# A hybrid decoder layer on one core: the 16-row solves of the chunk inverse along each partition's own row, in an order searched anew

## The chip, the core and the metric

The kernel runs on one core of a Trainium2 chip. A core has five engines with an instruction stream of their own each, which run their instructions in the order given: TensorE (PE, matrix products; PEld is its loading of weights), VectorE (DVE), ScalarE (ACT), GpSimd (POOL) and SyncE (SP), which here does nothing but issue transfers (DMA). The metric is the device time of one execution in microseconds (us). The profile and the trace come from one execution that the hardware profiler recorded.

## The reference

One layer of a decoder over 2048 tokens of width 1024 (`D_MODEL`). The token mixer is a gated DeltaNet of 8 heads of 128, next to a memory attention of 4 heads; then an output projection, two layer norms and a squared-ReLU MLP (1024 to 4096 and back). The part that the change touches is the chunked recurrence of the mixer:

```python
decay = jnp.exp(jnp.where(causal, gc[..., :, None] - gc[..., None, :], -jnp.inf))
lower = jnp.where(strict, jnp.einsum('bnhcd,bnhsd->bnhcs', k_beta, kc) * decay, 0.0)
a_mat = jnp.eye(CHUNK, dtype=f32) + lower
u = lax.linalg.triangular_solve(a_mat, v_beta, left_side=True, lower=True, unit_diagonal=True)
w = lax.linalg.triangular_solve(a_mat, k_beta * jnp.exp(gc)[..., None], left_side=True,
                                lower=True, unit_diagonal=True)
...
v_new = u_c - jnp.einsum('bhcd,bhde->bhce', w_c, state)
o = jnp.einsum('bhcd,bhde->bhce', qd, state) + jnp.einsum('bhcs,bhse->bhce', a_c, v_new)
state = state * dc[..., None, None] + jnp.einsum('bhcd,bhce->bhde', kd, v_new)
```

`q` and `k` are convolved, passed through SiLU and normalized per head; the output `o` is normalized by its root mean square and gated.

## The kernel before

The tokens go in four blocks of 512 (`TB`). In each block the mixer runs over the 8 heads, so that there are 32 pairs of block and head; `NC` = 4 chunks of 128 tokens make a block. Per pair, `dense` (L948) projects `cq`, `ck`, `cv` (products `aq`, `ak`, `av` of the input `T` with weights `whl`), convolves and gates them on DVE, squares them for the norms (`ss`) and works out small per-token factors on GpSimd: `rk`, `vbs`, `bh`, `nbe`, `e` (`e4`). `gdn_a` (L1125) makes the masked decays `dl` and `at` from `gb`, the products `pkq`, and multiplies them in, with `bh`; `invert` (L1004) inverts the four unit lower triangular 128x128 matrices I + L: first the 16-row blocks on the diagonal by substitution on DVE, then 16 to 32, 32 to 64 and 64 to 128 by pairs of small matmuls `pq` and `pp`, with the result in `Y`. `gdn_b` (L1183) runs the recurrence over the chunks (`pc`, `R`, `vt`, `po`, the state), then the norm (`oss`, `m`, `ro`), the transposition `pto` and the gate `cat`.

In the substitution the block's columns lie across partitions: `Lc` and `Xc` have 16 rows x 4 chunks along a partition. Step j spreads column j over a group of 16 partitions with a shuffle, multiplies it by one column of `Lc` and subtracts:

```python
for j in range(15):
    w = j + 1
    nc.vector.stream_shuffle(B[:, :w], Xc[:, :w], [j] * 16 + [16 + j] * 16)
    nc.vector.tensor_tensor(out=B[:, :w], in0=B[:, :w],
                            in1=Lc[:, j:j + 1].to_broadcast([P, w, NC]), op=ALU.mult)
    nc.vector.tensor_tensor(out=Xc[:, :w], in0=Xc[:, :w], in1=B[:, :w], op=ALU.subtract)
```

All large products are made of three fp32r matmuls on a high and a low part (`mm3`, the low parts by an ACT cast and a DVE subtract); the small ones of the inverse and the recurrence are fp32 matmuls. The out projection and the MLP use seven products for eight of half the size. The order in time is: mixer of blocks 0 and 1 (to about 640 us), out projection (to about 760), MLP (to about 1330), mixer of blocks 2 and 3 (from about 1390 to about 1940, about 1190 us of mixer in all), out projection (to about 2075), MLP (to the end).

Every operation of every engine is recorded first (`Recorder`) and then issued in the order of a table of numbers, `ORDER`, read by `order()` (L484) in `issue()` (L539), so that all of them have the line L549 in the trace. The table interleaves the pieces of a head with the projections of others, on each engine. Buffers come from pools of fixed number (four weight buffers `whl`, 14 slots of one kind for `gb`, `dl`, `at`, `Y` and the like); a transfer waits until its buffer is free.

Of the kernel before, what the change touches and what calls it, by code (L numbers as in the profile page):

```python
# [11 lines left out]
ALU = mybir.AluOpType  # L12
# [158 lines left out]
class Op:  # L171
# [4 lines left out]
    "c-rlK+m7ryuH+A;0qZXP|BsF0LfKiX*6!U8Gr$0iK4-72s!XS?3q=Nl!TZxb>Fa;vbCplke-?gmt@c^{bEO+U<$J%%e5d|8Cx5v1b@rduep%Y*"  # L176
    "!aJ^V^H1ed@TXGwRr{}H?Q87+>_6ah<&!3Uv0voIPw|&{cdq+(a=Ue{JO8-X=YLo4_;0E|e!p<L<Nd4sZJ(O=9kd%S^<Uh7>YuqEbDja&pWAQR"
    "cT#bC`_lWVu6<AY&dR<3o}$e0X}DO$jaG~jK3+0!yZ!ZcfBoP7bX^}`sEz$^FH_g5ciq3iNbhfIpS&<jt#DrUsO|sZZu6dteaHJ!_x$7XIsMa@"
    "UpberH?QB`wx=uafxh<F;tp2V{Pr8aZ=ZVeRy&uBK2p~HOeuBG?7kv~td4sR`ox3mk?o&eu~MdQV?PDHq@1s;{B6O^x5NS37p+=eHG9P--tLuj"
    "Ke^(5_IKgMzZ?4tUw~<@`$p=(eBWGjTH<vt0o?k``(ZKUcxTxIzjs0z{8oIX@8w%+;q~?#unjPIX|Mjob(gq#_WKJ~(tgN_B~ub-vGjuFv+p0*"  # L180
    "%9VQ%tDx*R=C*%V2EI<$ANz^17we~#j<5bNR@xpn4*H%lJx=F7%+rsCUk*%a&HK%G!P{sWslj>OPrX-o|7gSIS-p(*_Q53P#oNE~p6!fbyZ?*("
    "%lfC|rmlf~x9==3OuxRNW6NRs_YCb7MC;<o-wSc>5nM7Y*WL&FUHELCdn@DF@eEwKyvKn#n_(fkmOZDf?U8Qdr$O0^40{qQq{E1815+?JFhP4M"
    "VyrMpSp$Wiw^`Z0ygwuRseGZSEv%ogx%b6z+dcO$!?quwr}A2=xW`UI$ysUp`b8EO6S4;&-dynYnHGERn~}I`GjEE6muSugE%08G`%(9}?JwNB"
    "b?s~JEAMsnwj}$>_8-#T`>FG)^W0GUuQdMZZTiaVX)5Om_J8gb-|zsHyL{jO{{E%QH7=KoJ=gbl?0;ZSVSccCN*y{)_$e&^sr9&$c3kF7U->a^"
    "iP!sjmZ=*}`W-9|J|H{TxDxiy+z^vz*tKoU9?AjpHtxoIyc*8|O!ofnhQ~>Jv3Cw+;v(Q7um==_pZV|;AK`OuL)fr}_WC(52A1~NciLdv+cu=V"
    "$N26gsar4FYI~aaV*O#v*RyQ%`rY1Rt)+Zcb^E0LPg`>6*shq&H8g)%@%yItVYQkp2Y=Xi$=CZP_@HnawhOTh3|DQD3D;V#T;XF6H+IUzD#bHi"
    "_-D26qu{sO%2|h3{$W7I_t_R(2S-RQG%y_-pjTL#vhS_6ire2u()Kd;A;wJ!!v!OeCYD--(b<czby^4PttLC4ZklK8js2U<cf-Vwh3j#}FJ8Fe"
# [1885 lines left out]
```

## Time and profile before

| | us |
|---|---|
| runs | 2701.4, 2702.3, 2703.96 (median 2702.3) |
| profiled execution | 2702.34 |
| its span in the trace | 2700.6 |
| PE busy | 2679.2 (99%) |
| DVE busy | 2128.6 (79%) |
| ACT busy | 1640.6 (61%) |
| POOL busy | 425.8 (16%) |

The profiled execution's own time is 1.7 us more than its span, which runs from the first to the last instruction. Busy time is an average over stages with different limits, and an engine that is busy for less than the span may still be waited for at some places. The rows that matter stand below the change.

### The profile page before, as it was taken

To read this page: it belongs to the slowest core of one execution; us is meant where nothing else is said; L and a number is where in the kernel's file an instruction comes from. 1 tells how busy PE (TensorE), PEld (TensorE's weight loads), DVE (VectorE), ACT (ScalarE), POOL (GpSimd) and SP (SyncE) were. 2 spreads that over 40 slices of the span, in tenths; PEclk is the share of its full clock that TensorE was granted. 3 is DMA by queue.
4 is the path that set the end of the run, shared out by engine and by line. 5 is a ranking of instruction groups with operands and counts; after the bars stand their busy time and mean duration, and the time that the engine had idled before them with its cause. 6 is when DMAs were issued, how large, how long until landed. Compare 5 with 4: busy or idle time off the path is not lost.

```text
span 2700.6 us, 42572 instructions
## 1 busy us (share of the span) xinstructions
PE 2679.2 (99%) x13553; PEld 2248.0 (83%) x13553; DVE 2128.6 (79%) x5658; ACT 1640.6 (61%) x4128; POOL 425.8 (16%) x1023
## 2 busy tenths in 40 slices
PE   9999999999999999999999999999999999999998
PEld 7888888888888888888888888888888888888887
DVE  7999889998877776766788887999978666567485
ACT  7778767786575555333446777777756555544342
POOL 3233233331000000000012322332201000000011
PEclk9999999999999999999999999999999999999999
DMA  8767558877888888789785434545678654486673
GB/s 296 267 212 282 182 184 289 310 252 266 280 297 291 302 292 290 284 291 296 236 300 198 154 134 163 181 150 184 211 266 282 216 175 148 152 291 217 209 238 121
DMA packets 222896, 633.73 MB, mean 235 GB/s; under 512 B 25648, under 2 KB 34256, under 8 KB 203728
## 3 DMA queue, kind: packets, MB, share of 16 engines
q1 hardware_dynamic: 222240, 630.97, 67.9%
q8 instruction: 107, 1.75, 0.3%
q14 instruction: 117, 0.96, 0.1%
q10 hardware_dynamic: 432, 0.05, 0.0%
HBM read 446.83 MB, written 184.09 MB: 234 GB/s over the span
## 4 chain that ended last, share of the span: by engine, by line
PE 91%; DVE 4%; DMA 2%; ACT 1%; issue 1%; POOL 0%; SPq 0%; POOLq 0%; DVEq 0%; ACTq 0%
PE fA L549 13%; PE f2A L549 12%; PE ao L549 8%; PE f2C L549 6%; PE fC L549 6%; PE az L549 6%; PE av L549 6%; PE ak L549 6%; PE aq L549 5%; PE f2B L549 3%; PE fB L549 3%; PE pc L549 3%; PE amq L549 3%; PE po L549 2%; PE pkq L549 1%; PE pq L549 1%
## 5 line engine op out<-in xcount | busy, mean ns | idle before, releaser
L549 ACT CAST whl<-wraw 128x512 fp32r<-128x512 f32 (+2 forms) x294 | 225.9, 779 | 194.4 <-PE fC L549 54.2
L549 DVE TENSOR_TENSOR whl<-wraw,whl 128x512 fp32r<-128x512 f32 (+2 forms) x294 | 257.9, 887 | 95.0 <-ACT whl L549 90.1
L549 PE MATMUL fA<-B,whl 128*128 128x512 f32 x1152 | 291.4, 390 | 0.0
L549 PE MATMUL f2A<-whl,X 128*128 128x512 f32 x1152 | 264.7, 390 | 0.0
L549 PEld LDWEIGHTS fA<-B,whl 128*128 128x128 f32 x1152 | 216.4, 188 | 44.9
L549 PEld LDWEIGHTS f2A<-whl,X 128*128 128x128 f32 x1152 | 216.3, 188 | 44.8
L549 ACT CAST X<-X 128x1024 fp32r<-128x1024 f32 x118 | 123.2, 1050 | 171.4 <-DMA X<-xsc 129.5
L549 PE MATMUL av<-T,whl 128*128 128x512 f32 x768 | 224.7, 406 | 0.0
L549 PE MATMUL ak<-T,whl 128*128 128x512 f32 x768 | 220.2, 404 | 0.1
L549 PE MATMUL aq<-T,whl 128*128 128x512 f32 x768 | 217.3, 403 | 2.7 <-ACT whl L549 1.2
L549 DVE TENSOR_TENSOR X<-X,X 128x1024 fp32r<-128x1024 f32 x118 | 143.5, 1220 | 82.7 <-ACT X L549 82.6
L549 PE MATMUL fC<-B,whl 128*128 128x512 f32 x768 | 199.3, 390 | 0.0
L549 PE MATMUL az<-T,whl 128*128 128x512 f32 x624 | 182.2, 405 | 0.0
L549 PE MATMUL f2C<-whl,X 128*128 128x512 f32 x768 | 177.0, 390 | 0.9 <-ACT X L549 0.9
L549 POOL TENSOR_SCALAR ve<-mv 128x1 f32<-128x1 f32 x34 | 20.5, 602 | 983.9 <-DVE mv L549 975.3
L549 PEld LDWEIGHTS f2C<-whl,X 128*128 128x128 f32 x768 | 144.2, 188 | 31.1 <-ACT X L549 1.3
L549 ACT CAST whl<-whl 128x1024 fp32r<-128x1024 f32 x92 | 96.7, 1052 | 119.5 <-DMA whl<-tsc 84.4
L549 PEld LDWEIGHTS fC<-B,whl 128*128 128x128 f32 x768 | 144.2, 188 | 29.9
L549 PEld LDWEIGHTS aq<-T,whl 128*128 128x128 f32 x768 | 138.5, 189 | 29.1 <-DVE T L549 2.0
L549 PEld LDWEIGHTS ak<-T,whl 128*128 128x128 f32 x768 | 138.2, 189 | 23.4 <-ACT whl L549 0.5
L549 PEld LDWEIGHTS av<-T,whl 128*128 128x128 f32 x768 | 137.3, 189 | 21.3 <-ACT ck L549 0.2
L549 DVE TENSOR_TENSOR whl<-whl 128x1024 fp32r<-128x1024 f32 x92 | 112.0, 1220 | 48.8 <-ACT whl L549 48.6
(305 smaller groups left out, 6437.5 us busy)
## 6 DMA issues: line engine op xcount, KB each, us to landing
whl<-wsc SPq DMA_DIRECT2D x100, 1024.0 KB, 5.4
wraw<-in_w_ff_dram SPq DMA_DIRECT2D x106, 512.0 KB, 4.7
X<-xsc SPq DMA_DIRECT2D x96, 512.0 KB, 5.0
wsc<-whl SPq DMA_DIRECT2D x36, 1024.0 KB, 6.5
whl<-tsc SPq DMA_DIRECT2D x64, 512.0 KB, 4.7
xsc<-hB SPq DMA_DIRECT2D x96, 256.0 KB, 3.5
xo<-cat SPq DMA_DIRECT2D x80, 256.0 KB, 5.3
wraw<-in_w_in_dram SPq DMA_DIRECT2D x35, 512.0 KB, 4.4
```

Of the source, the lines that this page charges most:

```text
L549: o.fn(*[res(a) for a in o.args], **{k: res(v) for k, v in o.kw.items()})
```

## The change

`invert`: The 16-row substitution runs along each partition's own row. `Lc` now holds, on each partition, I - L of its own row of the block (4 chunks x 16); it is stored to DRAM (`lscr`) and loaded back as two tiles `Lr` of 128 x 512, in which every partition of a group of 16 has all 16 rows of its block. Step j then is a product `Mc` of row j with what is solved so far, and a sum over it, which is entry j: no shuffle and no subtraction. The result comes out transposed, so that `ZT` is built first and `Z` by a transposition of it.

`dense`: `bh` is worked out on DVE from `ss` and `ib` = 1 + exp(-b), as the reciprocal of their product, without the power `rk`; the additions of the epsilons are made apart for k and q, the one of q in one operation with its factor. `gdn_b`: the factor 1/P moves into the squares on ScalarE, and one GpSimd operation per head goes. The table `ORDER` is another one.

```diff
+    nhalf = cst.tile([P, 2], F32, name="nhalf")
+    nc.vector.tensor_scalar_mul(nhalf, half, -1.0)
...
-        nc.gpsimd.tensor_scalar_add(ss, ss, 4 * RMS_EPS)
+        bh = res["bh"] = small("bh", [P, NC])
+        nc.vector.scalar_tensor_tensor(out=bh, in0=ss[:, :NC].part(0), scalar=4 * RMS_EPS, in1=G["ib"][:, h], op0=ALU.add, op1=ALU.mult)
+        nc.vector.reciprocal(bh, bh)
         rk = small("rk", [P, NC])
-        nc.gpsimd.tensor_tensor(out=rk, in0=ss[:, :NC], in1=mhalf, op=ALU.pow)
-        res["e4"] = small("e4", [P, NC], 4)
-        nc.gpsimd.tensor_scalar_mul(res["e4"], ss[:, NC:], P * RMS_EPS)
+        nc.gpsimd.tensor_scalar_add(rk, ss[:, :NC].part(0), 4 * RMS_EPS)
+        nc.gpsimd.tensor_tensor(out=rk, in0=rk, in1=mhalf, op=ALU.pow)
...
-        bh = res["bh"] = small("bh", [P, NC])
-        nc.gpsimd.tensor_tensor(out=bh, in0=G["beta"][:, h], in1=rk, op=ALU.mult)
-        nc.gpsimd.tensor_tensor(out=bh, in0=bh, in1=rk, op=ALU.mult)
+        res["e4"] = small("e4", [P, NC], 4)
+        nc.gpsimd.tensor_scalar(out=res["e4"], in0=ss[:, NC:].part(1), scalar1=4 * RMS_EPS, scalar2=P * RMS_EPS, op0=ALU.add, op1=ALU.mult)
...
-        Lc = small("Lc", [P, 16, NC], 2)
-        Lf = Lq.rearrange("p c f -> p f c")
-        nc.vector.tensor_scalar_mul(Lc, Lf[:, 0:16], half[:, 0:1])
-        nc.vector.scalar_tensor_tensor(out=Lc, in0=Lf[:, 16:32], scalar=half[:, 1:2], in1=Lc,
+        Lc = small("Lc", [P, NC, 16], 2)
+        nc.vector.scalar_tensor_tensor(out=Lc, in0=Lq[:, :, 0:16], scalar=nhalf[:, 0:1],
+                                       in1=i16.unsqueeze(1).to_broadcast([P, NC, 16]), op0=ALU.mult, op1=ALU.add)
+        nc.vector.scalar_tensor_tensor(out=Lc, in0=Lq[:, :, 16:32], scalar=nhalf[:, 1:2], in1=Lc,
                                        op0=ALU.mult, op1=ALU.add)
...
-        for j in range(15):
+        lscr = rec.buf(dr, (8, 16 * 16 * NC), F32, "lscr", 2, "lscr")
+        nc.sync.dma_start(out=lscr.rearrange("g (i f) -> (g i) f", i=16), in_=Lc.rearrange("p c f -> p (c f)"))
+        Lr = []
+        for n in range(2):
+            t = slot("Lr", "s0")
+            nc.sync.dma_start(out=t, in_=lscr[:, n * TB:(n + 1) * TB].unsqueeze(1).to_broadcast([8, 16, TB]))
+            Lr += [t.rearrange("p (i c f) -> p i c f", i=8, c=NC)[:, m] for m in range(8)]
...
+        for j in range(1, 16):
             w = j + 1
-            nc.vector.stream_shuffle(B[:, :w], Xc[:, :w], [j] * 16 + [16 + j] * 16)
-            nc.vector.tensor_tensor(out=B[:, :w], in0=B[:, :w],
-                                    in1=Lc[:, j:j + 1].to_broadcast([P, w, NC]), op=ALU.mult)
-            nc.vector.tensor_tensor(out=Xc[:, :w], in0=Xc[:, :w], in1=B[:, :w], op=ALU.subtract)
+            nc.vector.tensor_tensor(out=M[:, :, :w], in0=Lr[j][:, :, :w], in1=Xc[:, :, :w], op=ALU.mult)
+            nc.vector.tensor_reduce(out=Xc[:, :, j], in_=M[:, :, :w], op=ALU.add, axis=AX.X)
...
-            nc.scalar.activation(j, p3[:, c], AF.Square, accum_out=o[:, c:c + 1])
+            nc.scalar.activation(j, p3[:, c], AF.Square, scale=P ** -0.5, accum_out=o[:, c:c + 1])
...
-        nc.gpsimd.tensor_scalar_mul(m4, oss, 1.0 / P)
-        nc.gpsimd.tensor_tensor(out=m4, in0=m4, in1=e4, op=ALU.add)
+        nc.gpsimd.tensor_tensor(out=m4, in0=oss, in1=e4, op=ALU.add)
```

How the instructions stand on an engine is shown at three places (the numbers behind the names count buffers). On DVE, in the middle of a solve early in the program, the order before has this, a step of three operations with pieces of the next head's convolution (`cq`), of the state and of `R` between them:

```order
L549 STREAM_SHUFFLE Bc_2398<-Xc_2255 128x16
L549 TENSOR_TENSOR Bc_2398<-Bc_2398,Lc_2886 128x16
L549 TENSOR_TENSOR kq_2844<-ck_2388,kq_2834 128x512
L549 SCALAR_TENSOR_TENSOR cq_2977<-raw_2495,cw_96,cq_2977 128x512
L549 SCALAR_TENSOR_TENSOR state_2889<-state_2889,el_513,pc_2960 128x128
L549 TENSOR_TENSOR Xc_2255<-Xc_2255,Bc_2398 128x16
L549 STREAM_SHUFFLE Bc_2398<-Xc_2255 128x20
```

Now, on DVE in the mixer of block 2, at the place where the least work stands between `Lc` (whose store follows it on SP) and the first product `Mc`, the order has:

```order
L579 SCALAR_TENSOR_TENSOR Lc_16619<-Lq_16562,nhalf_86,Lc_16619 128x64
L579 TENSOR_SCALAR Y_15779<-pp_16611 64x2x64
L579 SCALAR_TENSOR_TENSOR cq_16584<-raw_16332,cw_98,cq_16584 128x512 x2
L579 SCALAR_TENSOR_TENSOR cat_16669<-pto_16645,gnwh_94,cz_15540 128x512
L579 SCALAR_TENSOR_TENSOR cq_16584<-th_16657,cq_16584 128x512
L579 SCALAR_TENSOR_TENSOR ck_16667<-raw_16570,cw_98,ck_16667 128x512 x2
L579 SCALAR_TENSOR_TENSOR R_16717<-pc_16673,nbe_16111,vb_16648 128x128
L579 SCALAR_TENSOR_TENSOR bh_16719<-ss_16685,ib_14951 128x4
L579 SCALAR_TENSOR_TENSOR ck_16667<-raw_16570,cw_98,ck_16667 128x512
L579 TENSOR_TENSOR Mc_16742<-Lr_16664,Xc_16153 128x4x2
L579 TENSOR_REDUCE Xc_16153<-Mc_16742 128x4
L579 TENSOR_TENSOR Mc_16742<-Lr_16664,Xc_16153 128x4x3
```

A step is two operations now, and the first one of a head needs what SP loads. SP's order for the same head is this, with weights `whl` and a kept gate `cz` around the new transfers, where it had weights and kept gates alone:

```order
L579 DMA lscr_16630<-Lc_16619 128x64
L579 DMA Lr_16664<-lscr_16630 128x1x512
L579 DMA whl_16675<-wsc_2257 128x2048
L579 DMA cz_16682<-zsc_15580 128x512
L579 DMA Lr_16689<-lscr_16630 128x1x512
L579 DMA whl_16696<-wsc_2395 128x2048
```

The first load stands directly behind the store that it reads, and the weights behind both. At the start of the program, on PE, the order before begins with matmuls on constants (`warm`):

```order
L549 MATMUL warm_106<-ones_80 128x128 x7
L549 MATMUL aq_124<-T0_118,whl_120 128x512
L549 MATMUL aq_124<-T1_122,whl_120 128x512
L549 MATMUL aq_124<-T0_118,whl_120 128x512
L549 MATMUL warm_106<-ones_80 128x128 x2
```

and now with the first projection:

```order
L579 MATMUL aq_139<-T0_130,whl_134 128x512
L579 MATMUL aq_139<-T1_136,whl_134 128x512
L579 MATMUL aq_139<-T0_130,whl_134 128x512 x2
L579 MATMUL aq_139<-T1_136,whl_134 128x512
L579 MATMUL aq_139<-T0_130,whl_134 128x512
L579 MATMUL aq_139<-T0_149,whl_134 128x512
L579 MATMUL warm_165<-ones_80 128x128 x10
```

Seven of the ten `warm` matmuls have moved from before the first `aq` matmul to behind the first seven of them.

## Rows read from the trace of the kernel before

**Rows 1.** The page's busy times of each engine, and the core's span and clock.

```profile
PE 2679.2 (99%) x13553; PEld 2248.0 (83%) x13553; DVE 2128.6 (79%) x5658; ACT 1640.6 (61%) x4128; POOL 425.8 (16%) x1023
...
core 0: 2700.6 us, clock 0.999
```

**Rows 2.** Busy us (instructions) in two stretches: PE, PEld, DVE, ACT, POOL; clock, DMA.

```profile
400.00:500.00 100.00, 97.80 (x562) 83.20 (x561) 93.01 (x355) 75.06 (x258) 34.78 (x85) 1.00 0.83 294
...
2690.00:2700.60 10.60, 2.52 (x12) 1.74 (x10) 6.34 (x10) 0.00 (x0) 2.63 (x3) 0.84 0.37 138
```

**Rows 3.** The chain that ended last, by engine.

```profile
PE 91%; DVE 4%; DMA 2%; ACT 1%; issue 1%; POOL 0%; SPq 0%; POOLq 0%; DVEq 0%; ACTq 0%
```

**Rows 4.** PE's waits, the eight longest: us in total, times, longest.

```profile
PE pto L549 <- ACT on L549: 1.8, 1, 1.8
PE pt L549 <- ACT st L549: 1.6, 1, 1.6
PE ptv L549 <- ACT Y L549: 1.2, 3, 0.5
PE warm L549 <- POOL mhalf L636: 1.2, 1, 1.2
PE pt L549 <- ACT e L549: 1.2, 2, 0.7
PE aq L549 <- ACT whl L549: 1.2, 1, 1.2
PE pp L549 <- ACT inv L549: 0.9, 3, 0.4
PE f2C L549 <- ACT X L549: 0.9, 1, 0.9
```

**Rows 5.** DVE by groups, the solve: out<-in, times, busy us, mean ns, idle.

```profile
L549 DVE TENSOR_TENSOR Xc<-Xc,Bc 128x4 f32<-128x4 f32 (+14 forms) x480 | 92.1, 193 | 5.5
L549 DVE TENSOR_TENSOR Bc<-Bc,Lc 128x4 f32<-128x4 f32 (+14 forms) x480 | 91.4, 192 | 5.8
L549 DVE STREAM_SHUFFLE Bc<-Xc 128x24 f32<-128x24 f32 (+13 forms) x480 | 88.9, 187 | 1.2
```

**Rows 6.** DVE by groups, the two reductions.

```profile
L549 DVE TENSOR_REDUCE mx<-sps 128x2 f32<-128x512 f32 x32 | 22.0, 686 | 4.4 <-PE sps L549 4.0
...
L549 DVE TENSOR_REDUCE gab<-pab 128x16 f32<-128x64 f32 x16 | 2.7, 212 | 0.1
```

**Rows 7.** POOL by groups, two of the factors' chain.

```profile
L549 POOL TENSOR_TENSOR rk<-ss,mhalf 128x4 f32<-128x4 f32 x32 | 36.2, 1132 | 2.2
...
L549 POOL TENSOR_TENSOR bh<-bh,rk 128x4 f32<-128x4 f32 x32 | 9.5, 296 | 1.8
```

**Rows 8.** Timeline, 439 to 446 us: start, us, engine; behind it the wait.

```profile
439.57 3.07 POOL L549 TENSOR_TENSOR m<-m,e 128x4 f32<-128x4 f32 x1
...
445.25 0.66 PE L549 MATMUL pto<-ident,on 128*128 128x128 f32 x4 [1.76 <-ACT on L549]
```

**Rows 9.** Transfers: count, KB each, median us from issue to landing.

```profile
whl<-wsc SPq DMA_DIRECT2D x100, 1024.0 KB, 5.4
...
gb<-scr SPq DMA_DIRECT2D x32, 256.0 KB, 4.9
...
scr<-gct SPq DMA_DIRECT2D x4, 16.0 KB, 3.0
```

**Rows 10.** SP's waits, 300 to 640 us: us in total, times, longest.

```profile
SPq L549 <- DMA wos<-wq: 11.5, 5, 4.4
```

**Rows 11.** Timeline of DVE, 439 to 443 us, a convolution step and R.

```profile
439.71 0.74 DVE L549 SCALAR_TENSOR_TENSOR cv<-raw,cw,cv 128x512 f32<-128x512 f32 x1
...
442.69 0.35 DVE L549 SCALAR_TENSOR_TENSOR R<-pc,nbe,vb 128x128 f32<-128x128 f32 x1
```

**Rows 12.** Timeline, one weight tile's issue and its first matmul.

```profile
502.97 0.46 SPq L549 DMA_DIRECT2D whl<-wsc  x1
...
517.32 0.48 PE L549 MATMUL az<-T,whl 128*128 128x512 f32 x1
```

More of the change, by code (lines that the diff above doesn't have):

```diff
@@ L476 @@
[L476 to L480 removed]
+    "c-ri}39jTi4lKGMCt%Ie{x|j&17+tqRkv?H;Nbxujq1K9N2e`I6d4Q#)4D#XUMcNA<x2ZmPFK0|e(A<rrCqt~7u!|v`hJ+kRqyLl%T=#3ueM(r"
@@ L917, in gates @@
         nc.vector.tensor_scalar_mul(G["neg"], eg, -1.0)
-        nc.vector.tensor_scalar_add(eb, eb, 1.0)
-        G["beta"] = small("beta", sh, 2)
-        nc.vector.reciprocal(G["beta"], eb)
+        ib = G["ib"] = small("ib", sh, 2)
+        nc.vector.tensor_scalar_add(ib, eb, 1.0)
+        beta = small("beta", sh, 1)
+        nc.vector.reciprocal(beta, ib)
         G["betah"] = small("betah", sh, 2)
-        nc.vector.tensor_scalar_mul(G["betah"], G["beta"], 0.5)
+        nc.vector.tensor_scalar_mul(G["betah"], beta, 0.5)
         pt = bank("pgt", "m")
@@ L984, in dense @@
                 nc.scalar.activation(j, pt[:, c * P:(c + 1) * P], AF.Square,
-                                     accum_out=ss[:, n * NC + c:n * NC + c + 1])
+                                     accum_out=ss[:, n * NC + c:n * NC + c + 1].part(n))
             if nm == "k":
@@ L1034, in invert @@
-        Z = small("Z32", [P, NC, 32], 2)
-        for hf in range(2):
-            nc.vector.tensor_scalar_mul(Z[:, :, 16 * hf:16 * hf + 16], Xc.rearrange("p f c -> p c f"),
-                                        half[:, hf:hf + 1])
-        Xr = small("Xr", [P, 16, 2], 1)
-        nc.vector.stream_shuffle(Xr, Xc[:, :, 2:4], list(range(16, 32)) + list(range(16)))
+        lscr = rec.buf(dr, (8, 16 * 16 * NC), F32, "lscr", 2, "lscr")
+        nc.sync.dma_start(out=lscr.rearrange("g (i f) -> (g i) f", i=16), in_=Lc.rearrange("p c f -> p (c f)"))
@@ new lines, in invert @@
+        Lr = []
[3 more added lines that the diff above has]
+            Lr += [t.rearrange("p (i c f) -> p i c f", i=8, c=NC)[:, m] for m in range(8)]
+        Xc = small("Xc", [P, NC, 16], 2)
+        nc.vector.tensor_copy(Xc, i16.unsqueeze(1).to_broadcast([P, NC, 16]))
+        M = small("Mc", [P, NC, 16], 2)
+        for j in range(1, 16):
+            w = j + 1
+            nc.vector.tensor_tensor(out=M[:, :, :w], in0=Lr[j][:, :, :w], in1=Xc[:, :, :w], op=ALU.mult)
+            nc.vector.tensor_reduce(out=Xc[:, :, j], in_=M[:, :, :w], op=ALU.add, axis=AX.X)
@@ L1040, in invert @@
+        ZT = small("ZT32", [P, NC, 32], 2)
+        for hf in range(2):
+            nc.vector.tensor_scalar_mul(ZT[:, :, 16 * hf:16 * hf + 16], Xc, half[:, hf:hf + 1])
+        Z = small("Z32", [P, NC, 32], 2)
+        nc.vector.transpose(Z.rearrange("p c f -> p (c f)"), ZT.rearrange("p c f -> p (c f)"))
         Xp = small("Xp", [P, 2, 16], 1)
-        nc.vector.scalar_tensor_tensor(out=Xp, in0=Xr.rearrange("p f c -> p c f"), scalar=half[:, 1:2],
-                                       in1=Z[:, 0:2, 0:16], op0=ALU.mult, op1=ALU.add)
@@ L1043, in invert @@
-        ZT = small("ZT32", [P, NC, 32], 2)
-        nc.vector.transpose(ZT.rearrange("p c f -> p (c f)"), Z.rearrange("p c f -> p (c f)"))
+        nc.vector.stream_shuffle(Xp, Z[:, 2:4, 0:16], list(range(16, 32)) + list(range(16)))
+        nc.vector.tensor_tensor(out=Xp, in0=Xp, in1=Z[:, 0:2, 0:16], op=ALU.add)
         XB, LB, X32, X64, Q, ZP, QP, N3 = (inv[n] for n in ("XB", "LB", "X32", "X64", "Q", "Z64", "Q64", "N"))
```

642 lines of the change are left out of this document (334 added, 308 removed).

## The prediction

> **What bounds the kernel now.** I read the busy times first. TensorE (PE) is busy for 2679.2 of 2700.6 us, VectorE (DVE) for 2128.6, and the TensorE clock was granted at 0.999 over the whole core [rows 1], which is the upper of its two levels (2.4 GHz). Nothing on the other engines can therefore give back more than PE's own idle time, 2700.6 - 2679.2 = 21.4 us, unless it takes matmuls away. Next, by stage: in the poorest stretch of the mixer that I read PE still works 97.80 of 100 us, with DVE at 93.01; and in the last 10.6 us PE works 2.52, so 8.1 us of the 21.4 are the tail behind the last matmul [rows 2]. The chain that ended last says the same: 91% PE, 4% DVE, 2% DMA, 1% ACT [rows 3]. So the question is not what DVE saves, but which of PE's waits end on something that the change makes earlier or later.
>
> The list of PE's waits [rows 4] names them. Three belong to the start and the feed-forward (warm 1.2, aq on its first weight 1.2, f2C 0.9), and pt on st 1.6 and on e 1.2 to the transpositions between the out projection and the feed-forward. The others, pto 1.8, ptv 1.2 and pp 0.9, are the mixer's, where DVE and GpSimd (POOL) set the pace: 3.9 us together. The eight rows sum to 10.0; with the tail of 8.1 that leaves 21.4 - 18.1 = 3.3 us in smaller waits and seams, partly the mixer's too. **Hence the ceiling of what shorter DVE and POOL work can give: 3.9 us by the named rows, 7.2 if all of the rest went as well.**
>
> **The matmuls.** Counted in the order of both kernels, the same 12,471 matmuls of the same shapes are issued, so PE's 2679.2 us stay. They stand in another order, and pass between the two matmul kinds (fp32 pieces of the solve, fp32r products) 23 times more often; I take that as nothing.
>
> **The 16-row solve on DVE.** Before, each of 32 solves has 15 steps of shuffle, multiply and subtract, 480 of each: 88.9, 91.4 and 92.1 us [rows 5]. Now a step is a multiply and a reduce. The multiply keeps its 192 ns. For the reduce the trace has two nearby rows: 212 ns for 64 inputs per partition and 686 ns for 512 [rows 6]. The new reduces read 8 to 64 inputs, so the first row is the near one: 480 x 0.212 = 101.8 us. Shuffle and subtract go: 88.9 + 92.1 - 101.8 = 79.2 us saved on DVE. The far row would make it 480 x 0.686 = 329 us, a loss of 148, but it is for eight times our largest input; I keep it only as a part of the slower rival. Off comes what moves to DVE: bh as two four-element operations per head, 64 x 0.19 = 12 us at the price of the small operations above (92.1 us over 480). The gather of Lc and the assembly of Z keep their number within one instruction. So DVE loses some 67 us, in about 1190 us of mixer, 93% busy to about 87%. On the path of PE this is worth nothing by itself: it shortens queues in front of instructions that PE waits for, worth a part of the 3.9.
>
> **POOL.** The scale bh, which the solve's input dl needs, stood behind rk's power (1132 ns) and two products, 296 ns the second [rows 7]; it now takes two DVE operations and no POOL one: at least 1132 + 2 x 296 - 2 x 193 = 1.3 us earlier per head. m loses one POOL operation. What such a POOL chain costs when it goes wrong is seen once: m<-m,e took 3.07 us at 439.57, and pto waited 1.76 us for what follows it [rows 8]. One 3.07 us operation thus explains nearly half of the 3.9. The slow one lies under DVE operations that read two SBUF tensors (cv<-raw,cw,cv at 439.71 [rows 11]). *The Trainium skill*, page "SBUF — State Buffer", section "Who interferes with whom", says that a DVE instruction with two SBUF inputs holds the port it shares with GpSimd against a GpSimd instruction that reads SBUF; this row agrees with it, in that it is slow beside them. By that rule the change would cut such DVE instructions (480 subtracts become reduces, which have one input), and the stall should be rarer, not gone, since the 512-wide ones remain.
>
> **The new transfers.** Lc goes to DRAM (32 KB) and comes back as two 256 KB tiles Lr, per head, all on SyncE's (SP) one queue: 96 more transfers, 32 x 32 KB + 64 x 256 KB = 17 MB. A store of 16 KB from SBUF took 3.0 us to land, a 256 KB load of the same kind 4.9 [rows 9]; with issue (0.46 for a transfer of 1 MB [rows 12], 0.3 each for these taken): 3.0 + 0.3 + 4.9 + 0.3 = 8.5 us from Lc to the first multiply, where before there was nothing in between. What covers it is DVE work issued between Lc and that multiply. In the tightest place (shown with the change) it is seven 512-wide operations, Y, R and bh: 7 x 0.74 by the row of cv, and three small ones of 0.2 to 0.35, about 6.0 us [rows 11]. The same reckoning for all 32 heads, by the mean durations of the same operations less their overlap, gives 5.4 to 13.4 us, median 8.0. So on about half of the heads DVE arrives up to 3 us before its factors, and then waits, in order, with R, state and Y copies queued behind it; on the other half nothing happens. The expected stall is thus some 16 x 1.5 = 24 us of DVE, smaller than the 67 us of work that left it. I take its effect on PE as +0.5 us, with bounds 0 and the slower rival.
>
> *The Trainium skill*, "DMA: Bandwidth & Descriptors", section "Rules for kernel authors", says that a transfer whose slowest dimension is below 16 uses at most that many of the 16 DMA engines; Lr's source has 8 groups outermost. No row of before has such a load. If the rule holds, an estimate goes by size: 1024 KB landed in 5.4 us where 256 KB took 4.9 [rows 9], so half the engines should add 0.5 us or less, a little more stall, no change of sign.
>
> SP: Lr must wait for lscr to land, so SP stands about 3 us per head with loads of weights behind it. SP does wait for a transfer's landing now, wos on wq, five times, at most 4.4 us [rows 10], without PE noticing. A weight tile is issued at 502.97 and its first matmul is at 517.32, 14.3 us later, for a landing of 5.4 [rows 9, 12]: 9 us of slack against 3 us of delay. I price it at nothing; where the slack is used up, the delay shows as a wait of aq, ak, av or az on whl.
>
> **Start.** The seven warm matmuls ahead of the first aq move behind aq; PE's first 5 us wait for data anyway. Between 0 (hidden) and +1.2 us (the warm row of rows 4, if the ten warm ones now stand in the path); I take +0.5.
>
> **Sum.** Of the mixer's waits (3.9 us, 7.2 at most, 0 at least) I take 3.5: the pto wait, by the shorter POOL chain, half of ptv and pp, and a fifth of the unnamed rest. -3.5 + 0.5 + 0.5 = -2.5 us against the profiled run's 2702.34 us (1.7 us more than its span), which is the median of the runs, 2702.3. **Forecast 2699.8 us**, 0.1% less: within 0.2% (5.4 us), about what a measurement of this kernel can tell from no change. Its own range is 2697 to 2703.5 (the ceiling of the named waits and a little of the rest gone, or nothing gained and the start's whole 1.2 lost).
>
> **Rivals.**
> 1. *DVE's relief clears the mixer's waits* and no cost shows: 3.9 and half or all of the 3.3, so -5.5 to -7.2 us, 2695 to 2697; 2696 taken. For it: DVE at 93% is the engine that is short there, and the PE work between the last pkq matmul and the first pq, in which the solve must fit, is 32.4 us at the median instead of 37.0 by the rates of PE's rows, so the order trusts a faster solve. Against it: that room was shortened with the solve, so waits may simply return.
> 2. *The round trip stalls DVE in the wrong place* (slower). The first multiply waits up to 3 us, and R behind it feeds a pc chain with about 1 us of matmuls between its links. The POOL stall of 3.07 us reached PE as 1.76 (57%) [rows 8]. 24 us of stall at 57% are 14 us, less the 2.5 gained: 2714; at half of that stall, 2707. It decides from a landing of Lr near 10 us after Lc, or if the reduces cost nearer to 686 than to 212 ns.
> 3. *SP's wait makes weights late*: 32 x 3 us of SP time; if two or three tiles came 2 us late, +5, and 2704; ten such, +20. Against it the 9 us above.
> 4. *Nothing happens*: the waits that go are replaced by equal ones in the new order: 2702.
>
> **How the numbers follow.** Forecast and rival 4 together 0.44, rival 1 0.36, rivals 2 and 3 0.20. Rival 1 lies on the bound, and a twentieth of the whole is put to its upper side; rivals 2 and 3 leave 0.02 under +0.2%. Faster by over 0.2% (under 2696.9): 0.31; within 0.2%: 0.44 + 0.05 + 0.02 = 0.51; slower: 0.18. The range is 2691 to 2710: below, the ceiling of 7.2 (2695.1) and as much again as the three transposition and feed-forward waits hold (3.7), should the new order happen to clear them; above, rival 2 at half its price and some. About 0.1 lies on each side.
>
> **What would show it.** PE busy unchanged within 2 us; DVE busy near 2060; reduces Xc<-Mc near 0.2 us; no 3 us GpSimd operation ahead of ro, and the pto wait gone; a wait of DVE's Mc on a DMA of Lr, under 2 us each and on half of the heads at most. The prediction is wrong if PE's waits name DVE's R, ZT or Xp chain (pq, pc, ptv) with more than 5 us, if whl shows up as a wait of ak, av or az, if PE's busy time moves by more than 5 us, or if DVE waits for Lr by more than 30 us in sum.

## The result, and the profile after

The changed kernel took 2709.89 us in the median of 8 runs (2707.69 to 2711.03), the kernel before 2701.98 in 8 runs beside it: a ratio of 1.0027 [1.0016, 1.0038] (here and below with its 95% interval), or 7.3 us more on 2702, with about 3 us to either side. Where times are compared below, a ratio is taken times 2702, so that runs on different chips stand on one scale. The profiled execution has a span of 2709.0 us, 8.4 more than before.

The page's busy times, as in [rows 1], and the chain by engine, as in [rows 3]:

```profile
PE 2686.9 (99%) x13553; PEld 2243.3 (83%) x13553; DVE 2093.6 (77%) x4763; ACT 1638.2 (60%) x4128; POOL 410.2 (15%) x927
...
PE 88%; DVE 5%; DMA 4%; ACT 1%; issue 1%; SPq 0%; POOL 0%; POOLq 0%; DVEq 0%; ACTq 0%
```

The granted clock is 0.999 again, the matmuls are as many, DVE, ACT and POOL are all busy for less time, and the kernel is slower. PE's idle time hardly moved, 2709.0 - 2686.9 = 22.1 us for 21.4; what rose by 7.7 us is its busy time. In the chain, DVE and DMA have 9% where they had 6%.

PE's waits, the eight longest (us in total, times, longest), as in [rows 4]:

```profile
PE aq L579 <- ACT whl L579: 5.2, 1, 5.2
PE pp L579 <- ACT inv L579: 1.9, 5, 1.0
PE sps L579 <- ACT mq L579: 1.2, 1, 1.2
PE ptv L579 <- ACT Y L579: 1.1, 4, 0.4
PE po L579 <- ACT vt L579: 0.6, 1, 0.6
PE pc L579 <- DVE R L579: 0.6, 1, 0.6
PE fA L579 <- DVE B L579: 0.5, 2, 0.3
PE pq L579 <- DVE YP L579: 0.4, 2, 0.2
```

The pto wait and the three of the transpositions and the feed-forward are gone. The 5.2 us of aq are the program's start, where the warm matmuls used to run; by the start of the matmul that has the same place in the count, PE is within 0.1 us of before at 100 us. So these rows do not hold the loss. The waits of PEld, the loading of weights ahead of each matmul, show shorter ones; these are rows of the recurrence and of the inverse, for the kernel before, then, with two of the out projection, for the one after:

```profile
PEld ptv L549 <- ACT Y L549: 5.6, 14, 0.9
...
PEld pc L549 <- DVE R L549: 1.2, 4, 0.6
...
PEld pc L549 <- DVE state L549: 0.9, 5, 0.2
```

```profile
PEld ptv L579 <- ACT Y L579: 5.3, 12, 0.8
...
PEld pc L579 <- DVE R L579: 3.5, 12, 1.0
PEld pp L579 <- issue: 3.3, 8, 0.7
PEld pc L579 <- DVE state L579: 2.8, 13, 0.3
...
PEld ao L579 <- DVE whl L579: 1.3, 5, 0.5
...
PEld ao L579 <- ACT whl L579: 0.7, 2, 0.4
```

The links of the recurrence (`pc` waiting for `R` and for `state`) are late three times as often, 25 times instead of 9. Many of these delays are a few tenths of a microsecond or less. They are 4.2 us of the increase; summed over all its rows, PEld waits 54.1 us in 136 places where it waited 40.4 in 87, while PE's idle time grows by 0.7 us: in this trace the short waits lie inside PE's busy time. The last two rows are new too: `ao`, the out projection, waits for its weights. By the starts of the matmuls, the mixers lose 4.6 us between 100 and 700 us and 3.5 between 1300 and 2000; out projections and MLP together lose nothing.

DVE's groups of the solve, as in [rows 5] (times, busy us, mean ns, idle before and what ended it), and the first of POOL's `m`, as in [rows 8] (least, median and longest ns):

```profile
L579 DVE TENSOR_TENSOR Mc<-Lr,Xc 128x20 f32<-128x20 f32 (+14 forms) x480 | 97.4, 204 | 11.9 <-DMA Lr<-lscr 2.2 <-DVE Xc L579 0.3
L579 DVE TENSOR_REDUCE Xc<-Mc 128x4 f32<-128x20 f32 (+14 forms) x480 | 89.8, 188 | 9.4
```

```profile
L579 POOL TENSOR_TENSOR m<-oss,e x32: 190/200/1108, 134.9 to 2008.3; 128x4 f32<-128x4 f32 x32
```

The steps cost 187 us of DVE for 272 before, and DVE waits 2.2 us in all for `Lr`, in two places. SP's waits, as in [rows 10] (here over the whole program), have a new row:

```profile
SPq L579 <- DMA lscr<-Lc: 40.3, 29, 4.4
SPq L579 <- DMA wos<-wq: 15.8, 6, 4.6
```

When the loads land can be worked out from the trace's semaphore updates: a transfer leaves 16 of them, an `Lr` load, as four small loads at the program's start, 9 (counted so, the updates of all eight semaphores come out exactly). The stores then land 1.4 us after their issue at the median. From the end of `Lc` to the landing of the first `Lr` it is 7.1 us at the median (5.4 to 13.3), to the first product 9.8 (6.9 to 16.2).

### The profile page after: what moved, and what is told of

Same layout as the page of the kernel before. It is cut to its first block, busy times and chain, and to the rows that moved or that the text cites. A ratio compares the mean times of both kernels' runs of the same rounds, so it can differ in the third digit from the quotient of the medians.

```text
span 2709.0 us, 41836 instructions
## 1 busy us (share of the span) xinstructions
PE 2686.9 (99%) x13553; PEld 2243.3 (83%) x13553; DVE 2093.6 (77%) x4763; ACT 1638.2 (60%) x4128; POOL 410.2 (15%) x927
## 4 chain that ended last, share of the span: by engine, by line
PE 88%; DVE 5%; DMA 4%; ACT 1%; issue 1%; SPq 0%; POOL 0%; POOLq 0%; DVEq 0%; ACTq 0%
PE f2A L579 13%; PE fA L579 12%; PE ao L579 7%; PE f2C L579 6%; PE fC L579 6%; PE ak L579 6%; PE aq L579 6%; PE av L579 5%; PE az L579 5%; PE f2B L579 3%; PE pc L579 3%; PE fB L579 3%; PE amq L579 3%; PE po L579 2%; PE pkq L579 2%; PE pq L579 1%
## 5 line engine op out<-in xcount | busy, mean ns | idle before, releaser
L579 PE MATMUL ao<-whl,X 128*128 128x512 f32 x528 | 143.0, 403 | 0.4 <-DVE f L579 0.3
```

The lines of the kernel that those rows point to most:

```text
L579: o.fn(*[res(a) for a in o.args], **{k: res(v) for k, v in o.kw.items()})
```

## The experiments

Three parts can be told apart: the new solve, its transfers, and the new order. Where a run reads a constant tile in place of the factors, its text says so, and its time stands for the work without those data.

**e1_no_transfers.** The new order without the transfers, which are recorded but not issued (`mute`).

```diff
+        rec.mute = True
...
-            Lr += [t.rearrange("p (i c f) -> p i c f", i=8, c=NC)[:, m] for m in range(8)]
+            Lr += [fac for m in range(8)]
```

> The changed kernel and its order, but the store lscr and the loads Lr are not issued; every product of the solve reads one constant tile of zeros instead (the inverse is not computed). Theory T (the round trip through DRAM costs the 8 us: SP's wait for the store, two more of the 14 slots, 17 MB of traffic): about 2700 us, the waits of pp and pc back near those of before. Theory O (the new order itself places work so that PE waits more in the inverse and the recurrence): 2707 to 2710, unchanged waits of pp, pc, po. Theory D (products and reduces cost DVE more than they show): 2707 to 2710 as well.

Measured: 2706.2 us, 1.0012 [1.0003, 1.0021], +3.2. About half of the loss goes with the transfers; without them the new order is still slower than before. PEld's waits for ptv, `state` and `R` stay about as large as in the kernel after (12.7 us together for 11.6):

```profile
PEld ptv L582 <- ACT Y L582: 5.4, 12, 0.8
...
PEld pc L582 <- DVE state L582: 4.7, 18, 0.6
...
PEld pc L582 <- DVE R L582: 2.6, 10, 0.7
```

**e2_old_order_new_solve.** The kernel before, its order kept, with the new step in the old one's places.

```diff
-            nc.vector.stream_shuffle(B[:, :w], Xc[:, :w], [j] * 16 + [16 + j] * 16)
-            nc.vector.tensor_tensor(out=B[:, :w], in0=B[:, :w],
-                                    in1=Lc[:, j:j + 1].to_broadcast([P, w, NC]), op=ALU.mult)
-            nc.vector.tensor_tensor(out=Xc[:, :w], in0=Xc[:, :w], in1=B[:, :w], op=ALU.subtract)
+        Lr = [fac] * 16
...
+            nc.vector.tensor_tensor(out=M[:, :, :w], in0=Lr[j][:, :, :w], in1=Xc[:, :, :w], op=ALU.mult)
+            nc.vector.tensor_reduce(out=Xc[:, :, j], in_=M[:, :, :w], op=ALU.add, axis=AX.X)
```

> The kernel before with its own order and its own GpSimd chain; only the solve's steps are replaced in their places: product with a constant tile and reduce for shuffle, multiply and subtract; no transfers (the inverse is not computed). It prices DVE's relief with the order held. Theories T and O: 2697 to 2701, a gain of 1 to 5 us. Theory D: at or above 2702.

Measured: 2698.45 us, 0.9983 [0.9974, 0.9992], -4.6. DVE's relief alone is worth that much. Its page:

```profile
PE 2677.3 (99%) x13553; PEld 2248.7 (83%) x13553; DVE 2068.5 (77%) x4699; ACT 1640.7 (61%) x4128; POOL 426.9 (16%) x1024
```

and rows of PE's waits, of PEld's, and of POOL's `m`:

```profile
PE pto L536 <- ACT on L536: 1.5, 1, 1.5
```

```profile
PEld ptv L536 <- ACT Y L536: 3.0, 7, 1.0
...
PEld pc L536 <- DVE state L536: 0.9, 5, 0.2
```

```profile
L536 POOL TENSOR_TENSOR m<-m,e x32: 195/204/2801, 135.0 to 1996.2; 128x4 f32<-128x4 f32 x32
```

Half of ptv's waits go; the wait of pto and the long GpSimd operation before it stay.

**e3_new_order_old_solve.** The reverse: the new order, with the old solve in the places of the new one and no transfers.

```diff
-            nc.vector.tensor_tensor(out=M[:, :, :w], in0=Lr[j][:, :, :w], in1=Xc[:, :, :w], op=ALU.mult)
-            nc.vector.tensor_reduce(out=Xc[:, :, j], in_=M[:, :, :w], op=ALU.add, axis=AX.X)
+            nc.vector.stream_shuffle(B[:, :w], Xc[:, :w], [j] * 16 + [16 + j] * 16)
+            nc.vector.tensor_tensor(out=B[:, :w], in0=B[:, :w],
+                                    in1=Lc[:, j:j + 1].to_broadcast([P, w, NC]), op=ALU.mult)
+            nc.vector.tensor_tensor(out=Xc[:, :w], in0=Xc[:, :w], in1=B[:, :w], op=ALU.subtract)
```

> The changed kernel and its order with the old solve (shuffle, multiply, subtract) in the places of product and reduce, and no transfers; the result is the reference's. Theory O: above the run without transfers by what the extra DVE work costs, 2710 to 2716. Theory T: 2700 to 2704, since the transfers are gone. Theory D: below the run without transfers.

Measured: 2796.39 us, 1.0344 [1.033, 1.0358], +93, far above every case that was expected. DVE is busy 85.5 us longer than in e1 (2182.1 for 2096.6), and the kernel takes 90 us longer. So the new order has room for the new solve and for next to nothing more: what the solve saves has been taken out of the room.

**e4_transfers_unread.** The kernel after, transfers issued as they are, the products reading the constant tile (the second half of e1's edit).

> The changed kernel and its order with all transfers issued, SP's wait for the store included, and the slots taken; only the products read a constant tile of zeros, so DVE never waits for Lr (the inverse is not computed). Theory T by traffic, slots or SP: about 2709, as the changed kernel. If DVE's wait for Lr alone were the cost: about 2700. Theory O: 2707 to 2710.

Measured: 2711.64 us, 1.0029 [1.0018, 1.004], +7.8: as slow as the kernel after. The transfers cost their 4 us without any product waiting for their data.

**e5_no_store_wait.** The loads read another piece of DRAM, so that SP doesn't stand until the store has landed.

```diff
-            nc.sync.dma_start(out=t, in_=lscr[:, n * TB:(n + 1) * TB].unsqueeze(1).to_broadcast([8, 16, TB]))
+            nc.sync.dma_start(out=t, in_=fscr[:, n * TB:(n + 1) * TB].unsqueeze(1).to_broadcast([8, 16, TB]))
```

> The changed kernel and its order with stores, loads, slots and DVE's reads of Lr; but the loads read another piece of DRAM, of zeros, that nothing writes meanwhile, so SP never stands behind the store (the inverse is not computed). If SP's wait for the store (40 us in 29 waits) is the 4 to 5 us that the transfers cost: 2705 to 2707, as without transfers. If it is the traffic or the slots: 2709 to 2712.

Measured: 2708.2 us, 1.0022 [1.0013, 1.0031], +5.9.

**e6_small_loads_unread.** The store's wait is kept, and the loads bring 16 of the 512 columns (`t[:, :16]`), unread.

> The changed kernel and its order with the store, SP's wait for it and the slots, but each load brings 16 instead of 512 columns (8 KB instead of 256 KB) and the products read a constant tile of zeros (the inverse is not computed). If the traffic of the loads costs the 4 to 5 us: 2705 to 2707. If SP's wait or the slots do: 2709 to 2712.

Measured: 2708.14 us, 1.0019 [1.001, 1.0028], +5.1.

**e9_slots_only.** Both together: small loads from the other piece, unread. What is left is the 96 issues and the two slots per head.

> The changed kernel and its order with stores and slots, but the loads bring 16 columns (8 KB) from a piece of DRAM that nothing writes meanwhile, and the products read a constant tile of zeros (the inverse is not computed): neither SP's wait for the store nor the loads' traffic is left, only the 96 issues and the slots. If traffic and SP's wait share the cost of the transfers: 2705 to 2707, as without transfers. If the slots or the issues cost: 2708 or more.

Measured: 2706.92 us, 1.0012 [1.0003, 1.0021], +3.2, the ratio of e1. So issues and slots cost nothing that can be measured in the new order. SP's wait for the store is 7.3 - 5.9 = 1.4 or 5.1 - 3.2 = 1.9 us, the bytes 7.3 - 5.1 = 2.2 or 5.9 - 3.2 = 2.7; the intervals of neighbours overlap, so that these halves are estimates. Their sum, 4.1 us, stands on ratios whose intervals (e1 and after) overlap a little, from 1.0016 to 1.0021; e4 and e1, which ran beside each other, differ by 5.4 us (2707.33 to 2714.45 against 2704.05 to 2708.56).

The traces speak for SP's part. PE's order is the same in these kernels, so that each matmul can be set against itself in e1. Between 640 and 1000 us, in the out projection and the MLP behind the first mixers, the three that wait for the store fall 3.1 (after), 2.5 (e6) and 1.7 us (e4) further behind e1, the two that don't 0.8 (e9) and 0.4 (e5); each is one execution.

**e7_old_order_new_solve_new_factors.** e2 with the new chain of small factors (`bh` on DVE, `e4`, `m4`; these edits are in the diff above).

> The kernel before with its order, the new solve on a constant tile without transfers (the inverse is not computed) and also the new chain of factors: bh on DVE, e and m with one GpSimd operation less. Theory O (the order costs the rest): 2696 to 2700, as with the new solve alone. If the move of bh to DVE costs: 2703 or more.

Measured: 2698.82 us, 0.9985 [0.9976, 0.9994], -4.1. The new factors are worth nothing measurable. The long operation on POOL moves on to `ro`, and pto still waits (1.1 us, on `on`); the tile view of `m` and what follows it:

```profile
L535 POOL TENSOR_TENSOR m<-oss,e x32: 199/202/688, 135.0 to 1998.0; 128x4 f32<-128x4 f32 x32
L535 POOL TENSOR_TENSOR ro<-m,mhalf x32: 1000/1014/3641, 136.2 to 1998.2; 128x4 f32<-128x4 f32 x32
```

**e8_new_order_five_steps.** e1 with only the first 5 of the 15 steps issued (`rec.mute = j > 5`).

> The changed kernel and its order without transfers, and only 5 of the 15 steps of each solve are issued (the inverse is not computed): 20 of 30 operations per head less, over 100 us of DVE work. If the new order costs because the solve's room is too short for DVE: 2695 to 2700, the waits of pc on R and of pp down. If it costs by where it places the pieces of the inverse and the recurrence among PE's matmuls: 2704 to 2707, hardly less than with all steps.

Measured: 2702.35 us, 0.9999 [0.999, 1.0008], -0.3. With 103 us of DVE work less than e1 the new order just reaches the kernel before, and stays 3.8 us behind e7, which does all the steps in the old order. So of the new order's 7.3 us (e1 against e7) some 3.5 go with DVE's work and some 3.8 with something else; the intervals make both estimates. That the 3.5 are lack of room is not shown by this run alone, since less work on DVE gains as much in the old order (e2: 4.6 us for 60). Summed over all rows, PEld waits 34.8 us in 78 places in e7, 43.0 in 112 here and 47.8 in 124 in e1. Rows of this run:

```profile
PEld pc L582 <- DVE state L582: 4.6, 16, 0.9
PEld ptv L582 <- ACT Y L582: 3.2, 8, 0.6
...
PEld pc L582 <- DVE R L582: 2.3, 9, 0.7
```

Against e1, ptv's fall with DVE's load, as in e2; the links of `state` and `R` don't.

**e10_links_first.** The kernel after, with 28 of these links moved ahead of a DVE operation of over 500 ns, as here:

```diff
-TENSOR_TENSOR pm<-pmT,pm 128x512
 SCALAR_TENSOR_TENSOR R<-pc,nbe,vb 128x128
+TENSOR_TENSOR pm<-pmT,pm 128x512
```

> The changed kernel, complete; in DVE's order 28 operations R and state that stood directly behind a long operation (over 500 ns) and were ready in its first half, or before, now stand ahead of it; nothing else moves but five ACT operations. If the new order costs because the recurrence's links stand behind long DVE operations (theory O, second half): 2706 to 2708, 2 to 4 us less than the changed kernel, with the waits of pc and po down. If it costs elsewhere: 2709 to 2711.

Measured: 2714.82 us, 1.0041 [1.0028, 1.0053], +11, outside what that theory expects: putting these links first gains nothing. PEld's waits for `R` are 4.5 us in 13 places, no fewer than the 12 of the kernel after.

**e15_new_order_small_later, e16_old_order_small_later.** The other side of the same idea: in the kernel after, 46 small matmuls that had been waiting are placed behind 75 projection matmuls; and, as its counterpart, 26 behind 46 in the kernel before, of which this is one.

```diff
-MATMUL pq<-YP,inv 128x64 x2
 MATMUL ak<-T,whl 128x512
 MATMUL az<-T,whl 128x512
+MATMUL pq<-YP,inv 128x64 x2
```

> The changed kernel, complete; in PE's order alone, 46 small matmuls for which PE waited over 60 ns in the profiled execution (13.1 us together; pp, pc, ptv, pq, po and the like) stand behind one to four projection matmuls (75 in all) that stood behind them; DVE, ACT, POOL and SP keep their order. If the new order costs because the small matmuls stand too close behind what they wait for: 2701 to 2706, 4 to 8 us less than the changed kernel. If the waits only move on to the next link of the chain: 2708 to 2711.

> The kernel before, complete, with the same edit of PE's order from its own trace: 26 small matmuls (10.2 us of waits) behind 46 projection matmuls. If room behind the producers is what PE's waits hang on: 2696 to 2700, faster than both kernels. If the waits move on: 2701 to 2704.

Measured: 2714.8 us, 1.0039 [1.0025, 1.0053], and 2705.12, 1.0009 [1.0, 1.0018]. Neither is faster than what it starts from (their intervals overlap or touch), and both lie far from the case in which room behind the producers is what the waits hang on.

**e11_new_order_outside_mixer, e14_new_order_outside_mixer_2.** Is the new order better in the out projections and the MLP? The kernel before's mixer order, with the late (e11) or all (e14) operations of these two parts in their new sequence.

```diff
-MATMUL ao<-whl,X 128x512
-MATMUL ao<-whl,xh 128x512
 MATMUL pc<-R,Y 128x128
 MATMUL ao<-whl,X 128x512
 MATMUL ao<-whl,X 128x512
-MATMUL ao<-whl,xl 128x512
+MATMUL ao<-whl,xh 128x512
```

> The kernel before, complete, with its own order in the mixer; the operations of the late out projection, of the norms and transpositions behind it and of the MLP stand among themselves as in the new order. The traces say that the new order takes 3.6 us of waits of pt and 1.0 of f2C away there: 2697 to 2700. If those waits hang on the profiled execution alone: 2702.

> The kernel before, complete, its own order in the mixer; all operations from the out projection to the end of the MLP, in both layers' halves, in the new order among themselves, set beside the mixer's by the matmul work that stands before each. The traces say that the new order takes about 4 us of waits of pt and f2C away there: 2697 to 2700. If that gain hangs on how the mixer ends: 2702 or more.

Measured: 2719.51 us, 1.0062 [1.0049, 1.0074], and 2789.69, 1.0311 [1.0297, 1.0325]. Neither answers the question: both kernels have waits that neither order has by itself (in e14 one wait of az for 9.4 us, pto 6.9, pgt 5.9).

**e12_old_order_transfers_15, e13_old_order_transfers_20.** The whole new solve with its transfers in the order of before. Of the 45 places of a solve the 30 steps take the last 30 (e12) or 25 (e13), to give the round trip time; what then lacked a slot was moved back, on PE and the other engines too.

```diff
-DMA wraw<-in_w_in_dram 128x1024 x3
+DMA wraw<-in_w_in_dram 128x1024
+DMA lscr<-Lc 128x64
+DMA Lr<-lscr 128x1x512 x2
+DMA wraw<-in_w_in_dram 128x1024 x2
```

> A complete kernel: the new solve with its store and its loads in the order of before; the 30 operations of a solve stand on the last 30 of the old 45 places, so that the first third of the room covers the round trip, and what lacks a slot is moved back until one is free (PE's order moves by 54 matmuls at most, in 618 places). Theory O with transfers at about 4 us: 2700 to 2704, at least 5 us under the changed kernel. If the round trip stalls DVE here, its cover is 4 to 14 us: 2705 or more, with a wait of Mc on Lr.

> The same with the solve's operations on the last 25 of the 45 places, so that the round trip has more cover (4 to 18 us) and the solve less room behind it. Theory O: 2700 to 2704 again; against the run before it this tells whether cover or room is short: less if DVE waited for Lr, more if the end of the solve comes late to PE (waits of pq and pp).

Measured: 2943.67 us, 1.0875 [1.0852, 1.0898], and 2972.92, 1.0997 [1.0982, 1.1012]: +236 and +269. PE's waits in e12:

```profile
PE ptq L532 <- ACT kd L532: 18.7, 15, 2.1
PE pkq L532 <- ACT jq L532: 18.4, 13, 1.7
PE pc L532 <- DVE R L532: 17.9, 15, 6.2
PE pp L532 <- ACT inv L532: 14.1, 6, 7.6
PE av L532 <- DMA whl<-wsc: 9.2, 5, 6.1
```

**e17_old_order_late_steps, e18_old_order_slots_small_loads.** Which part of e12 is it? e17 is e2 with the steps on e12's late places; e18 is e12's order and slots, with loads of 64 columns from the other piece of DRAM and no wait for the store.

```diff
-            nc.sync.dma_start(out=t, in_=lscr[:, n * TB:(n + 1) * TB].unsqueeze(1).to_broadcast([8, 16, TB]))
+            nc.sync.dma_start(out=t[:, :64], in_=fscr[:, n * TB:n * TB + 64].unsqueeze(1).to_broadcast([8, 16, 64]))
```

> The order of before with the new solve on a constant tile, without transfers or slots (the inverse is not computed), but its 30 operations on the last 30 of the old 45 places, where a round trip would have had its cover. If the old room is long enough for the trip: 2697 to 2701, as with the steps in their own places. If the late start costs: 2703 or more. Either way it prices the room apart from the slots.

> The kernel of e12 with its order and its two slots per head, but each load brings 64 columns (32 KB) from a piece of DRAM that nothing writes meanwhile, and all products read these (the inverse is not computed). If the slots are what breaks the order of before: 2850 to 2950, as e12. If SP's wait for the store and the traffic break it: below 2720.

Measured: 2699.58 us, 0.9981 [0.9972, 0.999], and 2874.07, 1.0629 [1.0615, 1.0644]: -5 and +170. Late steps cost nothing, so the old order has time in which a round trip could be made. What costs is in what e18 adds to e17: the two slots per head, out of 14 that `gb`, `dl`, `at` and `Y` share, the store and the loads in SP's queue, and the operations moved to make place for them. No run takes these apart. In e18 PE and SP wait as in e12, though no load waits for a store to land:

```profile
PE pkq L532 <- ACT jq L532: 18.5, 13, 1.7
PE ptq L532 <- ACT kd L532: 18.5, 15, 1.9
PE pc L532 <- DVE R L532: 13.7, 13, 3.9
```

```profile
SPq L532 <- DVE Lc L532: 112.8, 12, 19.1
SPq L532 <- DVE Mc L532: 104.6, 21, 13.4
```

The first row is the store, for which SP stands until DVE has made `Lc` (the kernel after has that row as well, 158.6 us in 25 places); in the second are more waits of the store, and some of `gb`. POOL's `at` and `dl`, which need `gb`, wait for the transfer that fills it:

```profile
L532 SPq DMA_DIRECT2D gb<-scr x32: 319/320/1886, 51.1 to 2052.4; - x32
...
  POOL at L532: 28.5, 4
  POOL dl L532: 18.5, 4
```

What stands behind such a wait in SP's queue waits as well: the longest of POOL's waits, 12.9 us, is for a `gb` behind a store for which SP had stood 13.4 us; others are for a `gb` that itself stood up to 19 us for its buffer. Of e12's 236 us, 170 are in e18 too; the other 66 go with the wait for the store's landing and the bytes. Part of both is the clock, granted at 0.968 in e12 and 0.977 in e18 over the core, that is, in some stretches at the lower of its two levels (1.2 GHz), in a kernel in which PE now waits.

## Why the prediction was wrong

It forecast 2699.8 us, no change within 0.2%; measured are 2709.89, slower. The account that the runs give, on the scale of ratios times 2702, each step with an interval of some 3 us to either side:

| step | predicted | measured | from |
|---|---|---|---|
| DVE's relief, order held | -3.5 | -4.6 | e2 |
| new chain of factors | (in it) | +0.5 | e7 against e2 |
| new order | 0, but for the start's +0.5 | +7.3 | e1 against e7 (e1 and e2, which ran beside each other: 7.8) |
| transfers | +0.5 | +4.1 | after against e1 (e4 and e1, beside each other: 5.4) |
| sum | -2.5 | +7.3 | |

**The step that failed first is the order.** "They stand in another order [...]; I take that as nothing" was said of the matmuls, and the mixer's gain was then added as if the order were the old one. With it fell "so PE's 2679.2 us stay": the same matmuls were busy for 2686.9 us, so that PE's idle time was no ceiling for what could be lost. The first rival had the fact at hand, that the room for the solve had shrunk from 37.0 to 32.4 us and that "waits may simply return", but the case made of it was an exact return, 2702. They came back with more than went: the same steps come to -4.6 us in the old order and to +3.2 in the new one (e2, e1). About half goes with DVE's work, since taking two thirds of the steps away gives 3.5 us back (e8); the prediction had read the shorter room as trust in a faster solve, where it is the solve's saving already spent (e3). The other 3.8 us lie in how the rest is placed. That they are the late links of `R` and `state` is argued from PEld's waits in after, e1 and e8, not shown: the one edit that put them first gained nothing (e10).

**The transfers were mis-sized, and for the wrong reason.** The prediction's 24 us of DVE stall and the second rival hung on DVE's wait for `Lr`; it is 2.2 us in two waits, and unread transfers cost the same (e4). The store landed in 1.4 us where 3.0 were taken, and DVE came to the first product 9.8 us behind `Lc` where 8.0 were taken, so that the data were nearly always there. "I price it at nothing", of SP's wait for the store, was too low by an estimated 1.4 to 1.9 us, though SP stood for only 40.3 us in 29 waits, 1.3 us per head where 3 were forecast. That fits the third rival's mechanism, at another place than it named: behind the start no weight tile is late at aq, ak, av or az, but in the out projections and the MLP PEld waits nine times for one, at ao, fA and fC, for 3.3 us together, in e1 four times for 1.3, and in before not once. The 2.2 to 2.7 us (an estimate as well) for 17 MB of traffic had no term at all. By *the Trainium skill*, "DMA: Bandwidth & Descriptors", section "Rules for kernel authors", a transfer whose outermost dimension is below 16 is confined to at most that many of the 16 DMA engines. The 9 updates per `Lr` load, in place of 16, fit it. A price is not to be seen: the loads landed 5.9 us after their issue at the median, `gb`, of the same size, 6.0 in the same run.

**Right for the wrong cause.** The pto wait went, as predicted, but not by shorter POOL work: with less DVE work it stays at 1.5 us (e2), with the new chain at 1.1 (e7). It is gone in after and e1, but also in the old order with the old POOL chain when the steps come late (e17); what DVE does beside it differs in these, but which operation decides is not shown. The prediction had it as the largest piece of its 3.5; what the relief really shortened is ptv's waits and others too small to list. By *the Trainium skill*, "SBUF — State Buffer", section "Who interferes with whom", a DVE instruction with two SBUF inputs contends with a GpSimd instruction that reads SBUF; the prediction drew from it that stalls get rarer. They did not: with 480 such instructions gone a POOL operation still took 2801 and 3641 ns, and operations more than 0.5 us over the median of their group number 58 before, 64 in e2 and 60 in e7. Others with two inputs remain, so the rule itself is neither shown nor refuted.

**DVE's busy time** was to fall by 67 us to 2060; it fell by 35. Reduces took 188 ns (forecast 212) and products 204 (192), and summed over all groups DVE's operations lost 2375.0 - 2279.6 = 95 us. But busy time is a union, and operations overlap: by 2375.0 - 2128.6 = 246 us before and 186 after. In the old order the fall is 60 us (e2).

**What held**: PE is the bound, and the moved start costs little, 0.1 us at most (0.5 forecast). PE's busy time was named as the sign of error from 5 us on; it moved by 7.7.

Why a new order at all? Set into the old one as e12, e13 and e18 do it, the transfers cost 170 us and more. As far as these runs go, the order is the price of the way the factors are spread, and together they cost more than the shorter solve earns. No kernel here that computes the layer beats the one before; those that do (e2, e7, e17) read constant factors. Outside the mixer, where the waits of pt and f2C went, the new order gains: by matmul starts the execution of e1 wins 2.8 us on before's between 760 and 1300 us and 1.1 behind 2075, so that its mixers lose more than the sum shows. What in them costs the 3.8 us stays open.

## What to carry to other kernels

Price a re-searched order as a term of its own with both signs, by how much of the saving the new order has already taken out of the room of the shortened work; the same solve was worth -4.6 us in one order, and with the other order it came to +3.2. When TensorE is busy 99%, look for losses in the waits of its weight loads: here 7.7 us of the loss stood in its busy time and 0.7 in its idle time. And count the buffers that a new transfer needs and what is queued behind it, before counting whether its data come in time.

## What the hardware showed unasked

A load of `Lr` (256 KB, 8 pieces each spread over 16 partitions) occupies SP for 594 ns at the median, where the load of `gb`, also 256 KB, takes 387 in the same run and took 320 before, and it is 599 ns when it brings only 16 of 512 columns (e6): the issue's time does not go by the bytes.

```profile
L579 SPq DMA_DIRECT2D Lr<-lscr x64: 567/594/943, 75.5 to 1957.3; - x64
...
L579 SPq DMA_DIRECT2D gb<-scr x32: 319/387/1532, 47.8 to 1911.5; - x32
```

Two kernels with the same DVE operations, e7 and e1, have nearly the same sum over groups (2284.1 and 2285.9 us) and busy times of 2074.9 and 2096.6: how much neighbouring DVE operations overlap differs with their order. In the new order operations of one solve, each of which needs the one before, more often stand next to each other: a sum directly behind its product 261 times of 480 in e1 and 155 in e7, a product directly behind the sum before it 259 and 81 times. DVE's idle time before products and sums is 9.4 and 9.3 us in e1, for 3.2 and 5.9 in e7. That this is the reason is likely, but no run changes it alone.
